# A fourth feature tile's weight sums made in device memory, and the second projection's first forms opened one product later

## The chip, the cores and the metric

One Trainium2 chip, one of its cores. The metric is device time in microseconds for one execution; the time given for a kernel is the median of several runs. The engines are TensorE (PE, matmuls; PEld is its weight loading), VectorE (DVE), ScalarE (ACT), GpSimd (POOL) and SyncE (SP, which here only issues transfers). Each has its own queue, worked through in order.

## The reference

One layer of an encoder trunk on 1024 tokens of width 1024, in float32. What matters here is the order of its parts and the gated MLP in it:

```python
hn = rmsnorm(h, norm_mix_g[i])
z = hn @ w_in[i]                       # pooling mixer columns, then q, k, v
a = pool_mixer(u, pool_w[i], pool_b[i], pool_scale[i])
o = chunk_attention(q, k, v, rel_bias[i])
h = h + jnp.concatenate([a, o], axis=-1) @ w_out[i]
hn = rmsnorm(h, norm_ffn_g[i])
up = hn @ w_up[i]                      # 1024 x 5632
gt, val = up[..., :D_FF], up[..., D_FF:]
gt = causal_dwconv(gt, conv_w[i], conv_b[i])
h = h + (jax.nn.gelu(gt, approximate=False) * val) @ w_down[i]   # D_FF = 2816
hn = rmsnorm(h, norm_ple_g[i])
gate = jax.nn.sigmoid(hn @ w_ple_gate[i] + b_ple_gate[i])
h = h + gate * (p[i] @ w_ple[i])
...
return rmsnorm(h, final_g)
```

## The kernel before

Activations lie transposed, features on the 128 partitions and tokens along the free axis. Every float32 product is made of three matmuls (`mm3`, L130 to L132): each operand is split into a high part in the matmul's type and a low part that holds the rest. `split` makes the two, the high part on ACT (L135) and the low part on DVE (L136). So any operand costs one ACT and one DVE operation before PE can use it.

The stages in order: input projections and attention (about 0 to 282 us in the profile), in which attention steps i = 0 to 66 (64 pairs of a head and a block of 128 tokens, and three to drain) are interleaved with the remaining projections, and POOL does the windowed sums of the pooling groups 2 and 3 (L458 to L472); the output projection, with `mix` for each pooling group (282 to 337); the MLP's up-projection (380 to 801); its down-projection (801 to 1005); the last gate and the norm.

**The up-projection** goes over 22 feature tiles, `fi` = 0 to 21. Each tile's product is a 2 x 2 block product in Strassen's manner: seven products numbered 1 to 7 instead of eight, each of 4 x 3 matmuls of 128x512. `steps` gives their order, 1, 5, 2, 6, 3, 7, 4 for most tiles. The seven need, as weight operands, three quarters of the weights as they are (products 1, 2, 4) and four sums of quarters (5, 6, 3, 7). Products 6 and 7 share a PSUM bank: after product 6, L858 (`u2`, on DVE) reads the bank, and product 7 accumulates on. Behind product 3, L860 and L861 finish the gate branch, and `gate` (L879 to L882) runs the convolution and GELU; behind products 7 and 4, L864 to L867 finish the value branch; `values_in` (L885, L886) multiplies the two, and SP stores the tile's result to the device-memory tensor GD (L921). The result of an even tile lies in X, of an odd tile in F.

**Where the sums come from.** For tiles 0 to 2 (`by_load`, `UP_SUMS = 3`) the four sums are made ahead of time in device memory, in the tensors SD, and each of the seven operands is one load (L755). For tiles 3 to 21 the four quarters are loaded and POOL makes the four sums in SBUF (L759, 76 operations), the sums of product 6 and 7 on top of that of product 5. `prepare` splits an operand up to four products ahead. `fetch` asks for loads into 17 buffers of 128x512: five in F and twelve in X, which is opened after the fourth product, in the place of the tile TB. For the last tile only the five in F are used.

**The sums in device memory** are made in units. A unit is one feature tile of `w_up` (unit numbers below `UP_SUMS`) or one row block of `w_down` (the eleven numbers above). `weight_sums(u, part)` has six parts with eight transfers in all: copies, and transfers that add to what lies there, which POOL issues. The first `EARLY = 8` units are made during the attention, unit u's part at step i = 7 + 6u + 2 part (`sums_due`). There, a copy of one element on POOL (L566) makes the transfers wait for a result of the attention, and all is kept behind what POOL had before in program order. The other units are made during the up-projection, with POOL issuing the adding ones and SP the copies.

**The down-projection** is a block product of the same kind, with eleven row blocks for each of seven products. Its weight operands for products 5, 6, 3 and 7 are the units of `w_down`. Its operands go through the same `split`, into a ring of buffers in B. B takes the place of X, once everything that uses X is done, which ends with the store of tile 20's result. `ready(6)` asks for the first six pairs of loads and `formed(2)` splits the first two pairs: two ACT and two DVE operations each. Both are called from `first_steps`, a hook that runs after product 6 of the last feature tile. The later pairs are asked for and split in the main loop.

**What sets the order.** PE's queue is written in program order (`manual_schedule`). For the other engines a scheduler orders the queues when the kernel is built, from what it believes to be ready and from program order; `high_priority` lifts an operation by 60 places, and `keep_in_program_order` pins one behind what its engine had before.

Of the kernel before, what the change touches and what calls it, by code (L numbers as in the profile page):

```python
# [6 lines left out]
F32 = mybir.dt.float32  # L7
# [13 lines left out]
NF = FF // P  # L21
# [62 lines left out]
def trunk(tc, xT, pT, vecs, w_qk0, w_in, w_v, bias, counts, pool_w, w_out, w_up, w_down,  # L84
# [4 lines left out]
    with tc.tile_pool(name="sb", bufs=1) as sb, \  # L89
# [6 lines left out]
        def region(z, dt):  # L96
            a, b = spans[z]
            return sb.tile([P, (b - a) * 256], dt, name=f"R{z}", tag=f"R{z}")

        Rs = [region(z, F32R) for z in range(5)]  # L100
# [3 lines left out]
        small = sb.tile([P, 80], F32, name="small")  # L104
        PS = pp.tile([P, 8, 512], F32, name="PS")
        GD = dr.tile([NF, P, SEQ], F32, name="GD")
        UP_SUMS = 3
        SD = [dr.tile([NF // 2 + UP_SUMS, P, 512], F32, name=f"SD{n}") for n in range(4)]

        b_pool = tc.tile_pool(name="b1", bufs=1)  # L110
# [431 lines left out]
        def weight(k, i, j):  # L542
            return w_down[k + NK * (j - 1), :, (i - 1) * 512:i * 512]

        def quarter(fi, q):
            return w_up[fi, q[0], :, q[1] * 512:(q[1] + 1) * 512]

        def weight_sums(u, part, copies=pool):

            s1, s2, s4, s3 = [t[u] for t in SD]  # L550
            a11, a12, a21, a22 = [quarter(u, (i, j)) if u < UP_SUMS else weight(u - UP_SUMS, i + 1, j + 1)
                                  for i in range(2) for j in range(2)]
            todo = {0: ((s1, a21, None), (s3, a21, None)), 1: ((s1, a22, ALU.add), (s3, a11, ALU.add)),
                    2: ((s2, s1, None),), 3: ((s2, a11, ALU.add),), 4: ((s4, s2, None),), 5: ((s4, a12, ALU.add),)}
            for to, src, op in todo[part]:
                tc.keep_in_program_order(pool.dma_start(to, src, accum_op=op) if op else copies.dma_start(to, src))

        EARLY = 8

        def sums_due(i, wi):  # L560

            due = [(u, part) for u in range(EARLY) for part in range(6) if 7 + 6 * u + 2 * part == i]
            if due:
# [151 lines left out]

        by_load = range(UP_SUMS)
        plain = {1: (0, 0), 2: (0, 1), 4: (1, 1)}
# [122 lines left out]
        def keep(dst, bank, scale=1.0):  # L840
            with tc.high_priority(AHEAD):
                act.activation(dst, PS[:, bank], AF.Copy, scale=scale)

        def step(fi, n):

            x, y, z, w = firsts.get(fi, (0, 1, 2, 3))
            product({1: x, 2: x, 5: z, 3: z, 6: y, 7: y, 4: w}[n], n not in (2, 3, 7))
            if n == 1 and fi != 1:
                keep(np1, x, -1.0)
            elif n == 2 and fi:  # L850
                gate0(x)
                if fi in halved:
                    gate(fi, HS[0])
            elif n == 5:
                keep(rawd if fi == 1 else V[:, HS[1]], z)
            elif n == 6:
                with tc.high_priority(AHEAD):
                    dve.tensor_tensor(u2, PS[:, y], np1, ALU.add)  # L858
            elif n == 3:
                dve.tensor_tensor(G2, PS[:, z], u2, ALU.subtract)  # L860
                dve.tensor_tensor(G2, G2, rst[:, HS[1]], ALU.mult)  # L861
                gate(fi, HS[1] if fi in halved else slice(0, SEQ))
            elif n == 7:
                dve.tensor_tensor(V[:, HS[0]], PS[:, y], np1, ALU.add)  # L864
                dve.tensor_tensor(V[:, HS[1]], V[:, HS[0]], rawd if fi == 1 else V[:, HS[1]], ALU.subtract)
            elif n == 4:
                dve.tensor_tensor(V[:, HS[0]], PS[:, w], V[:, HS[0]], ALU.add)  # L867

        def gate0(bank):
            dve.tensor_tensor(Gb[:, 2:2 + 512], PS[:, bank], rst[:, HS[0]], ALU.mult)  # L870
# [13 lines left out]
        def values_in(y):  # L884
            dve.tensor_tensor(V, V, rst, ALU.mult)  # L885
            dve.tensor_tensor(y, y, V, ALU.mult)  # L886
# [15 lines left out]
        used += [False] * 12  # L902
        Ys = (X[:, 6144:7168], Yb)

        def up(fi, hook=None):
            if fi == 0:
                pool.memset(Gb[:, 0:2], 0.0)
                gate0(firsts[0][0])
            if fi == 1:
                keep(np1, firsts[1][0], -1.0)  # L910
            for n in steps[fi]:
                step(fi, n)
                if hook and n == 6:
                    hook()
            y = Ys[fi % 2]
            due = [(EARLY + z, fi - 4 - 2 * z - z % 2) for z in range(NK + UP_SUMS - EARLY)]
            due = [(u, part) for u, part in due if 0 <= part < 6]
            if any(part % 2 for _, part in due):
                tc.keep_in_program_order(pool.tensor_copy(small[:, 78:79], y[:, 0:1]))
            values_in(y)  # L920
            tc.keep_in_program_order(sp.dma_start(GD[fi], y))  # L921
            for u, part in due:
                weight_sums(u, part, sp)
# [18 lines left out]
        def weight_sum(n, k):  # L942
            return SD[SUM_OF[n]][UP_SUMS + k]

# [9 lines left out]
        def operands(n, k):  # L954

            z = {1: k - READY, 5: k + NK - READY}.get(n, -1)
            if 0 <= z < NK:
                load_to(B12(z), gated(z, 1, 2))
            if n == 1:
                return load_to(raw_buf(), weight(k, 1, 1)), load_to(T(k), gated(k, 1, 1))  # L960
            if n in (5, 6, 3, 7):
                if n == 5:
                    load_to(B22(k), gated(k, 2, 2))
                return load_to(raw_buf(), weight_sum(n, k)), {5: T, 6: T, 3: B22, 7: B12}[n](k)
            if n == 2:
                b21[k] = load_to(raw_buf("g"), gated(k, 2, 1))
                return load_to(raw_buf(), weight(k, 1, 2)), b21[k]
            return load_to(raw_buf(), weight(k, 2, 2)), T(k)
# [23 lines left out]
        READY, FORMED, LAG, LAG_1 = 6, 2, 4, 8  # L992
        got, made = {}, [0, 0]

        def ready(upto):
            while made[0] < min(upto, len(sequence)):
                got[made[0]] = operands(*sequence[made[0]])
                made[0] += 1

        def formed(upto):  # L1000
            while made[1] < min(upto, len(sequence)):
                i = made[1]
                w_, g_ = got.pop(i)
                (split_neg if sequence[i][0] in (5, 6) else split)(g_, *g_form[i % 3])
                split(w_, *w_form[i % 4])
                behind(*sequence[i])
                if i >= LAG and sequence[i - LAG][0] != 1:
                    later_sums(*sequence[i - LAG])
                if i >= LAG_1 and sequence[i - LAG_1][0] == 1:
                    later_sums(*sequence[i - LAG_1])  # L1010
                made[1] += 1

        g_form, w_form = [], []

        def first_steps():
            x_pool.__exit__(None, None, None)
            B = b3_pool.__enter__().tile([P, 7168], F32R, name="B3")
            g_form.extend((B[:, 1024 * s:1024 * s + 512], B[:, 1024 * s + 512:1024 * s + 1024]) for s in range(3))
            w_form.extend((B[:, 1024 * s:1024 * s + 512], B[:, 1024 * s + 512:1024 * s + 1024]) for s in range(3, 7))
            Rs[0] = region(0, F32)  # L1020
            ready(READY)
            formed(FORMED)

        b3_pool = tc.tile_pool(name="b3", bufs=1)
        for fi in range(NF):
            up(fi, first_steps if fi == NF - 1 else None)
        pinned[0] = True
        for z in (1, 2, 3):
            Rs[z] = region(z, F32)
# [241 lines left out]
```

## Time and profile before

| | |
|---|---|
| median of three runs | 1139.93 us (1139.84 to 1141.75) |
| the profiled execution | 1138.89 us |
| its span, first to last instruction | 1137.1 us |
| PE busy | 1121.7 us, 99% |
| DVE busy | 891.4 us, 78% |
| ACT busy | 577.9 us, 51% |
| POOL busy | 281.5 us, 25% |
| POOL's sums of quarters, L759 | 76, in up-projection, 1.29 to 2.34 us each |
| granted TensorE clock | 0.997 |

How to read it: a line of the timeline has the start, the duration, the engine, the line of the kernel, the operation, then written and read tiles with shapes, and in brackets how long the engine was idle before it and who ended that. A line of the waits has who waited, for whom, the microseconds in total, how often and the longest. SPq is SP's queue, where transfers are issued; the time of an issue is not the time of the transfer. Matmul times overlap, since a matmul starts before the one ahead of it has ended; the distance between two starts is the pace.

### The profile page before, as it was taken

What the parts mean: (1) busy time and instruction counts of PE and PEld (TensorE: products, weight loads), DVE (VectorE), ACT (ScalarE), POOL (GpSimd) and SP (SyncE); (2) the same over time, 40 slices, a digit from 0 to 9 for tenths busy, and PEclk for the clock granted to TensorE, in tenths of its full rate; (3) what the DMA queues carried; (4) which work ended last, traced back from release to release, by engine and by line L of the source; (5) the groups of instructions that cost most, each with busy time, mean ns of one, the idle gap of its engine ahead of it and who ended that gap; (6) DMA issues with size and microseconds to landing.
All of it is one profiled execution on the core that took longest, in us unless ns stands there. A gap on an engine that the chain in (4) does not pass through costs nothing.

```text
span 1137.1 us, 15326 instructions
## 1 busy us (share of the span) xinstructions
PE 1121.7 (99%) x5517; PEld 944.6 (83%) x5517; DVE 891.4 (78%) x1371; ACT 577.9 (51%) x1001; POOL 281.5 (25%) x297
## 2 busy tenths in 40 slices
PE   9999999999999999999999999999999999999996
PEld 7988998888888878888888888887888888888886
DVE  7678878779656788989898999988896688757344
ACT  8568677765554553434343434344444567545222
POOL 0013334275002213444463555333000000000000
PEclk9999999999999999999999999999999999999998
DMA  7134756534500343142635463414673564310012
GB/s 266 38 86 114 166 118 179 122 85 130 185 14 16 122 156 102 65 140 78 172 100 157 115 167 93 102 37 127 233 269 102 167 193 159 121 48 1 1 74 75
DMA packets 63340, 133.46 MB, mean 117 GB/s; under 512 B 7392, under 2 KB 9696, under 8 KB 62816
## 3 DMA queue, kind: packets, MB, share of 16 engines
q1 hardware_dynamic: 51664, 107.25, 28.5%
q0 software_dynamic: 9856, 23.07, 11.1%
q10 hardware_dynamic: 1744, 2.17, 0.5%
q8 instruction: 43, 0.70, 0.3%
q14 instruction: 33, 0.27, 0.1%
HBM read 116.73 MB, written 45.09 MB: 142 GB/s over the span
## 4 chain that ended last, share of the span: by engine, by line
PE 88%; DVE 6%; ACT 2%; issue 2%; DMA 1%; SPq 0%; DVEq 0%; POOLq 0%; POOL 0%; ACTq 0%
PE PS L130 27%; PE PS L132 27%; PE PS L131 27%; PE PS L370 2%; PE PS L387 1%; PE PS L388 1%; DVE R L136 1%; DVE B L378 1%; ACT F L356 1%; PE PS L344 1%; PE PS L345 1%; DMA F<-in_w_qk 0%; DVE F L346 0%; DMA R<-GD 0%; PE PS L353 0%
## 5 line engine op out<-in xcount | busy, mean ns | idle before, releaser
L130 PE MATMUL PS<-R,R 128*128 128x512 f32 (+1 forms) x932 | 359.7, 386 | 2.7 <-ACT R L135 1.4
L132 PE MATMUL PS<-R,R 128*128 128x512 f32 (+1 forms) x932 | 356.0, 382 | 0.0
L131 PE MATMUL PS<-R,R 128*128 128x512 f32 x868 | 338.1, 390 | 0.5 <-DVE R L231 0.5
L130 PEld LDWEIGHTS PS<-R,R 128*128 128x128 f32 x932 | 175.2, 188 | 35.5 <-ACT R L135 3.1
L132 PEld LDWEIGHTS PS<-R,R 128*128 128x128 f32 x932 | 175.1, 188 | 34.3 <-DVE R L136 0.2
L131 PEld LDWEIGHTS PS<-R,R 128*128 128x128 f32 x868 | 163.2, 188 | 33.0 <-DVE R L231 1.7
L132 PE MATMUL PS<-B 128*128 128x512 f32 x316 | 123.3, 390 | 0.1
L130 PE MATMUL PS<-B 128*128 128x512 f32 x316 | 123.3, 390 | 0.0
L131 PE MATMUL PS<-B 128*128 128x512 f32 x316 | 123.1, 390 | 0.0
L759 POOL TENSOR_TENSOR X<-X 128x512 f32<-128x512 f32 x42 | 80.2, 1912 | 122.9 <-DVE R L136 71.2
L136 DVE TENSOR_TENSOR R<-F,R 128x512 fp32r<-128x512 f32 (+1 forms) x117 | 94.0, 815 | 19.9 <-ACT R L135 19.4
L135 ACT ACTIVATE R<-F 128x512 fp32r<-128x512 f32 (+1 forms) x121 | 72.2, 613 | 72.1 <-PE PS L131 31.1
L135 ACT ACTIVATE R<-X 128x512 fp32r<-128x512 f32 x97 | 60.6, 629 | 86.0 <-PE PS L131 58.1
L136 DVE TENSOR_TENSOR R<-X,R 128x512 fp32r<-128x512 f32 x97 | 97.3, 1004 | 0.6 <-ACT R L135 0.6
L135 ACT ACTIVATE B<-F 128x512 fp32r<-128x512 f32 (+1 forms) x94 | 60.6, 646 | 70.6 <-PE PS L131 54.4
L659 POOL TENSOR_TENSOR small<-small 128x4 f32<-128x4 f32 (+1 forms) x7 | 8.1, 1158 | 336.2 <-DVE small L658 336.2
L136 DVE TENSOR_TENSOR B<-F,B 128x512 fp32r<-128x512 f32 (+1 forms) x94 | 66.6, 712 | 26.2 <-ACT B L135 25.9
L132 PEld LDWEIGHTS PS<-B 128*128 128x128 f32 x316 | 59.3, 188 | 12.9 <-DVE B L136 0.5
L131 PEld LDWEIGHTS PS<-B 128*128 128x128 f32 x316 | 59.4, 188 | 12.3
L130 PEld LDWEIGHTS PS<-B 128*128 128x128 f32 x316 | 59.4, 188 | 12.1
L131 PE MATMUL PS<-B,R 128*128 128x256 f32 (+1 forms) x208 | 64.1, 308 | 0.0
L759 POOL TENSOR_TENSOR F<-F 128x512 f32<-128x512 f32 x20 | 38.0, 1900 | 75.0 <-DVE R L136 34.9
(178 smaller groups left out, 2092.1 us busy)
## 6 DMA issues: line engine op xcount, KB each, us to landing
SD<-in_w_down POOLq DMA_DIRECT2D x54, 256.0 KB, 4.7
X<-in_w_up SPq DMA_DIRECT2D x53, 256.0 KB, 3.4
F<-SD SPq DMA_DIRECT2D x49, 256.0 KB, 2.7
R<-GD SPq DMA_DIRECT2D x44, 256.0 KB, 5.4
F<-in_w_down SPq DMA_DIRECT2D x33, 256.0 KB, 3.4
F<-in_w_up SPq DMA_DIRECT2D x32, 256.0 KB, 3.7
GD<-X SPq DMA_DIRECT2D x11, 512.0 KB, 3.3
GD<-F SPq DMA_DIRECT2D x11, 512.0 KB, 2.9
```

Source lines behind the costliest of these rows:

```text
L130: pe.matmul(ps, ahi, bhi, start=first, stop=False, skip_group_check=more)
L131: pe.matmul(ps, ahi, blo, start=False, stop=False, skip_group_check=more)
L132: pe.matmul(ps, alo, bhi, start=False, stop=last, skip_group_check=more)
L135: act.activation(hi, src, AF.Copy)
L136: dve.tensor_tensor(lo, src, rv(hi), ALU.subtract)
L344: pe.matmul(PS[:, 4 + z, 0:320], q, K2[:, ks], start=True, stop=False)
L345: pe.matmul(PS[:, 4 + z, 0:320], q, K1[:, ks], start=False, stop=True)
L356: act.activation(S[:, 0:n], S[:, 0:n], AF.Exp, bias=s_[:, 0:1], scale=-1.0, accum_out=s_[:, 1:2])
L370: pe.transpose(pst[:, j * P:(j + 1) * P], S[:, j * P:(j + 1) * P], ident)
L378: dve.tensor_tensor(lo, pst, rv(hi), ALU.subtract)
L387: pe.matmul(O, V[:, k, h], pt[:, 0, idx], start=n_ == 0, stop=False)
L759: pool.tensor_tensor(rawu[to], rawu[a], rawu[b], op)
```

## The change

Two edits. First, `UP_SUMS` goes from 3 to 4 and `EARLY` from 8 to 9. Feature tile 3 then takes its four sums from SD, by load, as tiles 0 to 2 do, and nine units are made during the attention: four of `w_up` and, as before, five of `w_down`. The added unit's place in the row pushes the later ones on, so the attention's parts reach to step 65 where they ended at step 59. In the up-projection the same six units of `w_down` are made in the same places as before, since both constants move by one.

Second, the hook is cut in two. `first_loads` (the region and `ready(6)`) stays behind product 6 of the last feature tile; `first_forms` (the end of X, the opening of B, and `formed(2)`) goes behind product 3, the next one.

```diff
-        UP_SUMS = 3
+        UP_SUMS = 4
...
-        EARLY = 8
+        EARLY = 9
...
-        def up(fi, hook=None):
+        def up(fi, hooks={}):
...
             for n in steps[fi]:
                 step(fi, n)
-                if hook and n == 6:
-                    hook()
+                hooks.get(n, lambda: None)()
...
-        def first_steps():
+        def first_loads():
+            Rs[0] = region(0, F32)
+            ready(READY)
+
+        def first_forms():
             x_pool.__exit__(None, None, None)
             B = b3_pool.__enter__().tile([P, 7168], F32R, name="B3")
             g_form.extend((B[:, 1024 * s:1024 * s + 512], B[:, 1024 * s + 512:1024 * s + 1024]) for s in range(3))
             w_form.extend((B[:, 1024 * s:1024 * s + 512], B[:, 1024 * s + 512:1024 * s + 1024]) for s in range(3, 7))
-            Rs[0] = region(0, F32)
-            ready(READY)
             formed(FORMED)
...
-            up(fi, first_steps if fi == NF - 1 else None)
+            up(fi, {6: first_loads, 3: first_forms} if fi == NF - 1 else {})
```

## The prediction

> **What bounds the kernel now.** I read the page first, then the waits of PE, then PE's timeline where those waits fall.
>
> ```profile
> span 1137.1 us, 15326 instructions
> PE 1121.7 (99%) x5517; PEld 944.6 (83%) x5517; DVE 891.4 (78%) x1371; ACT 577.9 (51%) x1001; POOL 281.5 (25%) x297
> ...
> PE PS L130 <- ACT R L135: 1.4, 1, 1.4
> PE PS L370 <- DVE B L378: 1.0, 3, 0.5
> PE PS L130 <- DVE F L858: 0.8, 1, 0.8
> ```
>
> PE is busy for all but 15.4 us of the span, and the change adds no matmul and takes none away. So it can only win back pauses of PE, or make new ones. Of the pauses listed in the waits, two lie in the gated MLP (L130, once each), which is where the change is at work; L370's three lie in the attention. PE's timeline shows the two with their sizes.
>
> ```profile
> 411.94 0.39 PE L132 MATMUL PS<-R,R 128*128 128x512 f32 x1
> 413.12 0.47 PE L130 MATMUL PS<-R,R 128*128 128x512 f32 x1 [0.78 <-DVE F L858]
> ...
> 793.59 0.39 PE L131 MATMUL PS<-R,R 128*128 128x512 f32 x1
> 793.82 0.39 PE L132 MATMUL PS<-R,R 128*128 128x512 f32 x1
> 795.57 0.47 PE L130 MATMUL PS<-R,R 128*128 128x512 f32 x1 [1.36 <-ACT R L135]
> ```
>
> Matmuls follow each other every 0.23 us (793.59 to 793.82). The first pause is 413.12 - 411.94 - 0.23 = 0.95 us, the second 795.57 - 793.82 - 0.23 = 1.52 us. Together 2.47 us: the most that the change can win in the MLP. A measurement of this kernel can tell about 0.2% from no change, here 2.28 us of 1139.93, so winning both pauses would just show and winning one would not. The profiled run took 1138.89 us, 1.79 beyond its span; the median of the three timed runs is 1.04 us above it. I take differences from the profile and put them on the median.
>
> **The first edit in the MLP: tile 3 without sums on POOL.** The first pause stands before product 7 of feature tile 1. That product accumulates into the bank of product 6, which L858 on DVE must read first, and L858 came late:
>
> ```profile
> 399.38 1.28 DVE L880 SCALAR_TENSOR_TENSOR X<-F,vec,X 128x1024 f32<-128x1024 f32 x1
> 401.18 2.32 DVE L881 SCALAR_TENSOR_TENSOR X<-F,vec,X 128x1024 f32<-128x1024 f32 x1
> 405.46 1.23 DVE L885 TENSOR_TENSOR V<-V,F 128x1024 f32<-128x1024 f32 x1
> 407.20 2.33 DVE L886 TENSOR_TENSOR X<-X,V 128x1024 f32<-128x1024 f32 x1
> 412.29 0.68 DVE L858 TENSOR_TENSOR F<-PS,F 128x512 f32<-128x512 f32 x1
> ...
> 401.03 1.38 POOL L759 TENSOR_TENSOR F<-F 128x512 f32<-128x512 f32 x1 [13.02 <-DMA F<-in_w_up]
> 406.84 1.60 POOL L759 TENSOR_TENSOR F<-F,X 128x512 f32<-128x512 f32 x1 [4.43 <-DVE V L885]
> 418.23 1.71 POOL L759 TENSOR_TENSOR X<-X 128x512 f32<-128x512 f32 x1 [9.79 <-DVE R L136]
> ```
>
> L881 takes 2.32 us where its twin L880 takes 1.28, and L886 2.33 where L885 of the same size takes 1.23. Under both slow ones runs a sum on POOL (L759). DVE loses 1.04 + 1.10 = 2.14 us there. Whose sums are these? SP's loads tell:
>
> ```profile
> 391.09 1.76 SPq L755 DMA_DIRECT2D X<-SD  x3
> 393.21 0.98 SPq L755 DMA_DIRECT2D X<-in_w_up  x2
> 394.86 6.75 SPq L755 DMA_DIRECT2D F<-in_w_up  x5
> 404.12 3.52 SPq L755 DMA_DIRECT2D X<-in_w_up  x2
> 410.16 8.33 SPq L755 DMA_DIRECT2D X<-in_w_up  x4
> ```
>
> The last three loads from SD are products 6, 3 and 7 of tile 2; the next load is its product 4. So loads run far ahead of the products, as fast as the 17 buffers come free. What follows is tile 3's quarters (one at 393, three of the five at 394.86), then tile 4's. The sum at 401.03 is therefore the first one of tile 3 (its operand of product 5), and that at 406.84 the first of tile 4. After the change tile 3 takes seven ready loads: one at 393, the five at 394.86 and one of the two at 404.12. Its four sums go. Tile 4's second and third quarters, which its first sum needs, move into the four loads of 410.16 (410.16 + 8.33 ends at 418.49), so that sum starts after 412 instead of at 406.84. Neither sum is left between 401 and 412.
>
> DVE's queue without them: L881 ends at 402.46; the four short operations behind it and L885 (1.23) then end by 405.6, L886 runs 406.2 to 407.4, and its successors move up by 2. L858 then starts near 410.3 instead of 412.29. PE wants the bank at 411.94 + 0.23 = 412.17. The pause of 0.95 us goes with 1.2 us to spare. If POOL's next sum came back under L886, half the gain of DVE would be lost and L858 would end near 411.9 (412.97 - 1.04): still in time, so I take the whole 0.95. What is late next is the operation that tile 4's sum then meets on DVE, near the place of the sum at 418.23; DVE has caught up 2 us by then. The bounds of this term are 0 (DVE keeps its delay for some other reason) and -0.95. Tile 3's three further loads cost SP 0.33 us each and lie beside PE; its three further sums, after 437, lie beside products that do not pause today.
>
> **The second edit: forms one product later.** Moved are eight instructions, two ACT and two DVE splits for each of two forms; the loads stay behind product 6, so SP passes nothing. The second pause again stands before a product 7, that of the last tile:
>
> ```profile
> 792.86 0.63 ACT L135 ACTIVATE B<-R 128x512 fp32r<-128x512 f32 x1 [1.69 <-DMA GD<-X]
> ...
> 793.52 0.69 DVE L136 TENSOR_TENSOR B<-R,B 128x512 fp32r<-128x512 f32 x1 [1.27 <-ACT B L135]
> 794.13 0.68 DVE L136 TENSOR_TENSOR B<-F,B 128x512 fp32r<-128x512 f32 x1
> 794.74 0.69 DVE L858 TENSOR_TENSOR F<-PS,F 128x512 f32<-128x512 f32 x1
> ...
> 797.87 0.69 DVE L136 TENSOR_TENSOR B<-R,B 128x512 fp32r<-128x512 f32 x1
> 798.47 0.69 DVE L861 TENSOR_TENSOR F<-F 128x512 f32<-128x512 f32 x1
> ```
>
> The waits name ACT, but L858 ends at 795.43 just as that ACT split does. Product 3's twelve matmuls end with the one at 793.82, so product 6 was done near 791.5 and L858 could have run from there. It stood behind two splits into B, and these waited for the store of tile 20 to leave X, whose place B takes. If the splits stood behind L858, the 1.52 us would go.
>
> But does a later place in the program put them there? The queue's order is not the program's. The split at 797.87 is the third form's, which the program writes after the whole last tile, and it stands ahead of L861, which belongs to that tile's product 3. The scheduler takes whatever it believes to be ready. The new place of X's closing does not hold B back either, if the pool before it is a guide:
>
> ```profile
> 387.06 0.69 DVE L136 TENSOR_TENSOR R<-TB,R 128x512 fp32r<-128x512 f32 x1
> 387.81 1.27 SPq L755 DMA_DIRECT2D X<-SD  x3
> 390.50 0.58 ACT L842 ACTIVATE V<-PS 128x512 f32<-128x512 f32 x1
> ```
>
> X was opened where TB was closed, behind the L842 that ran at 390.50; yet the first load into X left at 387.81, as soon as the last reader of TB had ended (387.75). So I expect the two forms to stay in front of L858, and this edit to be worth 0, with ends at -1.52 and, should they instead come too late for the second projection, +0.69 for one split.
>
> **The first edit in the attention: one more unit on POOL's queue.**
>
> ```profile
> L556 POOL DMA_DIRECT2D SD<-in_w_up x18: 546/845/1163, 71.0 to 144.0; - x18
> L556 POOL DMA_DIRECT2D SD<-SD x16: 502/562/946, 85.9 to 248.5; - x16
> L566 POOL COPY small<-F x27: 174/182/1040, 70.8 to 249.1; 64x1 f32<-64x1 f32 x27
> ...
> 251.83 0.85 POOL L556 DMA_DIRECT2D SD<-in_w_down  x1 [2.56 <-DMA SD<-SD]
> 271.42 0.70 POOL L472 TENSOR_TENSOR F<-F 128x240 f32<-128x240 f32 x1
> 276.46 1.06 ACT L135 ACTIVATE B<-F 128x1024 fp32r<-128x1024 f32 x1 [2.62 <-issue]
> 277.55 0.38 ACT L393 ACTIVATE F<-PS 64x256 f32<-64x256 f32 x1
> 288.83 0.50 PE L132 MATMUL PS<-B 128*128 128x512 f32 x1
> ```
>
> A unit is six transfers from the weights and two within SD: 6 x 0.845 + 2 x 0.562 = 6.2 us of POOL. Steps 55, 57 and 59 of the attention get a second part, and 61, 63 and 65 get a part and a copy (0.18 each, 0.5 together). One landing more is waited for on the way, as at 251.83 (2.56). All of it lies ahead of or among POOL's pooling of group 3, which now ends at 272.12. It would end near 272.1 + 6.2 + 0.5 + 2.6 = 281.4. PE uses that group only in the second `mix`, after 292, so the result itself is in time. The danger is ACT's split of it at 276.46, with L393 and the splits of the output weights behind it. That ACT could start only when the last product with PT was over, so today 4.3 us of cover lie before it (272.12 to 276.46). I expect the queue's order to shift with POOL's, and take 0. The bounds are 0 and +5.0 (281.4 - 276.46).
>
> One rule speaks against the edit. The Trainium skill, page "SBUF — State Buffer", section "SBUF: two separate sides", says that a transfer issued from POOL cannot have its descriptors written while DVE runs an operation in a two-port mode. The rows of L556 bear on it: 0.845 us at the median and 1.163 at the most, so eight issues at the longest would be 8 x 1.163 = 9.3 us instead of 6.2, and the sum above would read 284.5. The trace shows no more than these 0.32 us between the median and the longest of those issues, and none held for as long as a whole operation of DVE could hold it.
>
> **Sum.** -0.95 + 0 + 0 = -0.95 us: 1139.93 - 0.95 = 1139.0.
>
> **Rivals.**
> - *Both pauses go*, -2.47: 1137.5. The forms do move behind L858. For it: L858 is ready 2 us before the first split, and whatever changes that one order wins. Against it: the third form's place, ahead of L861. Chance 0.22.
> - *ACT stands still for POOL*, slower. The place is ACT's split at 276.46: if it stays ahead of L393 while POOL ends late, every microsecond of POOL after 276.46 holds L393 and the output weights, and PE has no slack at the first `mix` (288.83, already late). At 281.4 it costs 5.0 - 0.95 = +4.0: 1144.0. It shows as slower once POOL ends after 276.46 + 0.95 + 2.28 = 279.7. Against it: a scheduler that counts the new transfers can put L393 first. Chance 0.18, two thirds of it beyond 0.2%.
> - *It does not do what it should*: the first pause stays, because another sum of POOL or another order keeps L858 late: 1139.9. Chance 0.16.
>
> **How the numbers follow.** The forecast has 0.44. Faster by over 0.2%: nearly all of the first rival, 0.21. Slower: two thirds of the second, 0.12. The rest, 0.67, is the same. The range runs from below the first rival's 1137.5 by what a small stall of the attention (L370) may give, 0.5, to the second rival's milder half, +1.7: 1137.0 to 1141.6. About 0.1 is left out on each side, and the ends of the forms' term, -1.52 and +0.69, lie inside.
>
> **What would show it.** In the changed profile: no L759 between 395 and 412, L881 and L886 of tiles 0 and 1 at 1.3 and 1.2 us, no wait of PE for L858 near 413; 72 sums instead of 76. Near 795, the two splits into B still in front of L858 and a pause of 1.5 us; if L858 stands first there, the second step is wrong. POOL's last L472 near 281, and ACT's L393 of the last values ahead of the split of group 3. A PE pause near 283 to 289 would prove the second rival.

## The result, and the profile after

The changed kernel takes 1145.01 us (median of six runs, 1144.28 to 1149.31), the kernel before 1139.87 on the same chip: a ratio of 1.0052 (over all runs, not of the medians alone) with an interval of 1.0041 to 1.0062. It is slower, by 5.1 us between the medians, where 1139.0 was forecast; that is outside the range of 1137.0 to 1141.6. The profiled execution took 1144.28 us; first the head of its page, then its waits of PE.

```profile
span 1142.5 us, 15338 instructions
...
PE 1124.0 (98%) x5517; PEld 946.2 (83%) x5517; DVE 887.3 (78%) x1371; ACT 578.7 (51%) x1001; POOL 279.3 (24%) x304
```

```profile
PE PS L130 <- ACT B L135: 3.0, 1, 3.0
...
PE PS L130 <- DVE F L858: 1.3, 1, 1.3
```

The wait near 413 is gone, the one left for L858 is the pause before the last product 7, and a new one of 3.0 us stands on top. To see where the time went I cut PE's queue at four matmuls that both kernels have, and compare the stretches between them (starts from the timelines, in us):

| stretch of PE | before | after | difference |
|---|---|---|---|
| to the first matmul of the output projection | 282.64 | 283.63 | +0.99 |
| output projection (to the first L655) | 55.08 | 60.14 | +5.06 |
| norm and up-projection (to the first matmul that reads B) | 463.41 | 462.40 | -1.01 |
| down-projection | 204.05 | 204.06 | +0.01 |

So nearly all of the loss lies in the output projection, and the MLP won what it should. The four differences add up to 5.05 us; the spans differ by 5.4, and the other 0.3 lies behind PE's last matmul, where I didn't follow it. Of the +0.99 ahead of the output projection, 0.3 was there by 9.95 us, long before the first unit at 71 us. Another 0.3 came at 269.28, where PE's L370 starts just behind the end of DVE's L378 (269.22); a split ahead of that L378 took 1.16 us instead of 0.82. The last 0.4 came from 276.14 on, where PE's L388 starts just behind the end of the next L378 (275.27 + 0.82 = 276.09), and that one is late for the reason found below.

PE's timeline of the changed kernel in the output projection (start, duration, idle time before it in brackets), and the mean granted clock (the number after POOL's count) of the four microseconds that follow the wait:

```profile
288.88 0.39 PE L132 MATMUL PS<-R,R 128*128 128x512 f32 x1
292.24 0.50 PE L130 MATMUL PS<-B 128*128 128x512 f32 x1 [2.96 <-ACT B L135]
292.57 0.40 PE L131 MATMUL PS<-B 128*128 128x512 f32 x1
293.29 0.78 PE L132 MATMUL PS<-B 128*128 128x512 f32 x1 [0.32 <-DVE B L136]
293.86 0.63 PE L130 MATMUL PS<-B 128*128 128x512 f32 x1
294.29 0.63 PE L131 MATMUL PS<-B 128*128 128x512 f32 x1
...
296.42 0.56 PE L130 MATMUL PS<-R,R 128*128 128x512 f32 x1
296.81 0.40 PE L131 MATMUL PS<-R,R 128*128 128x512 f32 x1
```

```profile
292.00:296.00 4.00, 3.44 (x9) 2.45 (x10) 3.88 (x10) 2.95 (x6) 0.00 (x0) 0.67 0.89 242
```

The pause is 292.24 - 288.88 - 0.23 = 3.13 us. The next two gaps lose 0.10 and 0.49. Then PE goes at 0.43 us a matmul instead of 0.23: the seven steps from 293.29 to 296.42 take 3.13 us where 1.61 is the pace, 1.52 lost, and the step after them 0.16. Together 5.40. Before, the same place lost 0.37 (gaps of 0.49 and 0.34 around 288.83), so 5.03 is new, against 5.06 in the table. About a third of it (1.68 us) is the clock, not the wait.

What holds the matmul of 292.24? Followed backwards through the timelines of ACT, SP, DVE and POOL of the changed kernel:

```profile
291.55 0.63 ACT L135 ACTIVATE B<-F 128x512 fp32r<-128x512 f32 x1 [4.27 <-DMA F<-in_pool_w]
...
288.75 0.33 SPq L182 DMA_DIRECT2D F<-in_pool_w  x1
...
269.74 0.68 DVE L136 TENSOR_TENSOR R<-F,R 128x512 fp32r<-128x512 f32 x1
274.45 0.44 DVE L458 TENSOR_TENSOR F<-F 128x271 f32<-128x271 f32 x1 [4.04 <-POOL F L458]
...
272.26 2.16 POOL L458 TENSOR_TENSOR F<-F 128x269 f32<-128x269 f32 x3
```

and the same places in the kernel before:

```profile
284.29 0.33 SPq L182 DMA_DIRECT2D F<-in_pool_w  x1
...
270.20 0.45 DVE L458 TENSOR_TENSOR F<-F 128x271 f32<-128x271 f32 x1
...
267.26 2.47 POOL L458 TENSOR_TENSOR F<-F 128x269 f32<-128x269 f32 x3
```

All these sums come from one line, L458, which runs on POOL for groups 2 and 3 and on DVE for groups 0 and 1. They keep their partial sums in the same two scratch tiles, T1 and T2. The four sums of each part of group 3 go back and forth between the two; group 0 needs one sum for each part and writes it to T1, which POOL's last sum still reads. Before, POOL was done with T1 at 267.26 + 2.47 = 269.73, and DVE came at 270.20. After, POOL is done at 272.26 + 2.16 = 274.42, and DVE, free at 270.42, stands still for 4.04 us. Everything behind it on DVE is late by that or a little more (the next L458, beside POOL's last operations, takes 0.93 us instead of 0.42). The load of the mixer's weights leaves right behind the DVE split that empties its buffer, 4.46 us later than before; ACT's split follows it, and PE that. DVE cannot catch up, as a stretch of time of the kernel before shows (behind the length come the busy times of PE, PEld and DVE):

```profile
272.00:300.00 28.00, 27.91 (x128) 22.71 (x127) 27.25 (x53) 17.34 (x28) 0.12 (x1) 1.00 0.63 202
```

It works 27.25 us of 28 there. An engine at 78% over the span has 0.75 us of slack in this stage.

### The profile page after: what moved, and what is told of

Same layout as the page of the kernel before. It is cut to its first block, busy times and chain, and to the rows that moved or that the text cites. A ratio compares the mean times of both kernels' runs of the same rounds, so it can differ in the third digit from the quotient of the medians.

```text
span 1142.5 us, 15338 instructions
## 1 busy us (share of the span) xinstructions
PE 1124.0 (98%) x5517; PEld 946.2 (83%) x5517; DVE 887.3 (78%) x1371; ACT 578.7 (51%) x1001; POOL 279.3 (24%) x304
## 4 chain that ended last, share of the span: by engine, by line
PE 86%; DVE 5%; POOL 3%; ACT 2%; issue 2%; DMA 1%; SPq 0%; DVEq 0%; POOLq 0%; ACTq 0%
PE PS L130 27%; PE PS L131 27%; PE PS L132 27%; POOL F L458 2%; PE PS L370 1%; PE PS L388 1%; PE PS L387 1%; DVE R L136 1%; DVE B L378 1%; ACT F L356 1%; DMA F<-in_w_qk 1%; POOL F L472 0%; DVE F L346 0%; POOL F L471 0%; PE PS L655 0%
## 5 line engine op out<-in xcount | busy, mean ns | idle before, releaser
L356 ACT ACTIVATE F<-F,small 128x640 f32<-128x640 f32 (+2 forms) x64 | 44.4, 694 | 23.0 <-DVE small L354 15.4
```

Source lines behind the costliest of these rows:

```text
L356: act.activation(S[:, 0:n], S[:, 0:n], AF.Exp, bias=s_[:, 0:1], scale=-1.0, accum_out=s_[:, 1:2])
```

## The experiments

My theory after the first reading: the ninth unit's time on POOL holds DVE at the shared scratch, and this alone makes the loss. Rivals: the transfers or their traffic cost it; the forms' new place costs something; the fourth tile by load costs something. Shares are against runs of the kernel before on the same chip, with 95% intervals.

**The change taken apart: three runs.** One keeps only the cut of the hook.

```diff
-        UP_SUMS = 4
+        UP_SUMS = 3
...
-        EARLY = 9
+        EARLY = 8
```

> The second edit alone: three tiles by load and eight units in the attention as before, the forms opened behind product 3. Theory (the scheduler places the forms by readiness, not by program position): the two splits into B still stand ahead of L858 on DVE, PE pauses about 1.5 us before the last product 7, the time is that of before, 1139.9 within 0.5. Rival (the second edit costs part of the 5 us, by splitting later): 1141 or more, with a new pause near 800.

Measured: 1139.26 us, 1.0001 (0.9992 to 1.0010). The pauses near 413 and 795 are both there, 0.98 and 1.21 us (from start to start, less 0.23). The cut is worth nothing.

The next is the kernel before with `UP_SUMS = 4` alone, so that the ninth unit is made during the up-projection.

> Four tiles by load but eight units in the attention: the last unit of w_down that the attention made moves to the up-projection. Theory (the loss comes from POOL being late for the end of the attention, which here it is not): DVE does not wait for POOL near 270, the pause near 412 goes, 0.95 us faster than before, 1138.9 within 0.7. Rival (loading the fourth tile's sums is what costs): slower than before, near 1145.

Measured: 1140.13 us, 1.0005 (0.9996 to 1.0014). The first pause went as expected, but the one near 795 grew; PE's timeline:

```profile
793.85 0.39 PE L132 MATMUL PS<-R,R 128*128 128x512 f32 x1
796.24 0.47 PE L130 MATMUL PS<-R,R 128*128 128x512 f32 x1 [2.00 <-DVE F L858]
```

2.16 us against 1.52 before. So 0.95 was won and 0.64 lost, and what is left is too small to tell. Why it grew isn't settled: in the profiles that have this pause it lies between 0.96 us (nine units alone) and 2.16, so a part of it changes from one execution to the next.

The third is the kernel before with `EARLY = 9` alone: nine units during the attention, three of `w_up` and six of `w_down`.

> Nine units in the attention but only three tiles by load, forms as before. Theory: DVE waits about 4 us for POOL at its first sum of pooling group 0 (L458), PE pauses about 3 us at the first mix and runs slowly for some us behind it, and the pause near 412 stays: about 6 us slower than before, 1146 within 1. Rival (the fourth tile's loads cost): as before, 1139.9.

Measured: 1146.38 us, 1.0061 (1.0048 to 1.0074), with DVE's wait and PE's, from its timelines:

```profile
275.62 0.44 DVE L458 TENSOR_TENSOR F<-F 128x271 f32<-128x271 f32 x1 [5.54 <-POOL F L458]
...
290.02 0.39 PE L132 MATMUL PS<-R,R 128*128 128x512 f32 x1
293.27 0.50 PE L130 MATMUL PS<-B 128*128 128x512 f32 x1 [2.87 <-ACT B L135]
```

The whole loss comes with the ninth unit in the attention, and it comes with three feature tiles of `w_up` among the nine as with four.

**POOL's time without the transfers.** The kernel before, with eight fills of a free tile on POOL behind its work on group 2, and no ninth unit.

```diff
+            if g == 2:
+                for _ in range(8):
+                    later.append(lambda: tc.keep_in_program_order(pool.memset(f(12, 640), 0.0)))
```

> The kernel before, with eight memsets of 128x640 on POOL behind its sums of group 2, pinned there: POOL time alone, no transfer added, nothing else changed; they write a bias buffer that is no longer read. Theory: POOL comes some 4 to 5 us later to the sums of group 3, DVE waits for the shared scratch, PE pauses at the first mix: slower by as much as the changed kernel or more, 1143 to 1147. Rival (the transfers themselves, by their memory traffic): no loss, 1139.9.

Measured: 1146.61 us, 1.0063 (1.0050 to 1.0077). DVE's timeline shows the same wait:

```profile
276.24 0.44 DVE L458 TENSOR_TENSOR F<-F 128x271 f32<-128x271 f32 x1 [5.57 <-POOL F L458]
```

No transfer was added and no further landing waited for: POOL's lateness is enough.

**The shared scratch taken away.** The changed kernel, with two tiles of its own for group 0's sums (lines behind it move by one).

```diff
+            S1, S2 = (f(12, 272), f(13.0625, 272)) if g == 0 else (T1, T2)
...
-                src, dst, m, lo_ = u, T1, 1, 0
+                src, dst, m, lo_ = u, S1, 1, 0
...
-                    src, dst = dst, (T2 if dst is T1 else T1)
+                    src, dst = dst, (S2 if dst is S1 else S1)
```

> The changed kernel, with a scratch of its own for the sums of pooling group 0 on DVE, so that they no longer share the two scratch tiles with POOL's sums of group 3; same transfers, same POOL work. Theory (DVE waits for POOL to leave the shared scratch, and everything behind it on DVE's queue is late): the wait near 270 goes, and with it the pause of 3 us at the first mix: 1138.9 within 1. First rival (the eight transfers slow the loads of pool_w and w_out in memory): no gain, 1144 to 1146. Second rival (POOL late for group 3 itself holds ACT's split of it): no gain, 1143 to 1146.

Measured: 1142.68 us, 1.0030 (1.0018 to 1.0041). A miss: DVE's wait is gone, yet the kernel is still 3.3 us slower than the kernel before (1139.42 on this chip). Its timelines of DVE, POOL and PE:

```profile
270.37 0.87 DVE L459 TENSOR_TENSOR F<-F 128x271 f32<-128x271 f32 x1
...
273.40 2.27 DVE L136 TENSOR_TENSOR R<-F,R 128x512 fp32r<-128x512 f32 x2
...
269.08 2.75 POOL L459 TENSOR_TENSOR F<-F 128x269 f32<-128x269 f32 x3
...
274.16 2.89 POOL L459 TENSOR_TENSOR F<-F 128x269 f32<-128x269 f32 x3
...
288.50 0.39 PE L132 MATMUL PS<-R,R 128*128 128x512 f32 x1
291.17 0.50 PE L130 MATMUL PS<-B 128*128 128x512 f32 x1 [2.27 <-ACT B L135]
```

DVE starts on time (270.37), but its sum takes 0.87 us where it took 0.45 before (270.20), and two splits take 2.27. Now POOL works until 279.35, beside DVE, instead of ahead of it. PE's pause is 2.44 us, and the clock stays at full speed behind it. ACT's split of group 3 waits for POOL here, until 279.39, but that holds nothing that ends last: DVE doesn't stand still from 268.43 until its split for the first `mix` at 291.32. From its first sum to the L446 at 282.14 it takes 11.77 us where it took 8.71 before (270.20 to 278.91). These 3.06 us, and the 0.17 by which DVE began later, are the 3.23 us by which the load of the mixer's weights leaves late (287.52). So the slow operations make the loss that is left. Two causes were possible for the slow operations: POOL beside DVE, or the new place of the scratch. Two more runs tell them apart. The control is the kernel before with the same three lines.

> The kernel before, with scratch of its own for group 0's sums on DVE, nothing else. Control for the changed kernel with its own scratch. My theory (the slow DVE operations there come from POOL working beside them, not from the new place of the scratch): 1139.9, DVE's first sum of group 0 at about 270.2 and 0.45 us long, no new pause of PE. The rival (reading or writing the new place is slow): that sum at 0.7 us or more, DVE late by 2 to 3 us, 1142.

Measured: 1139.25 us, 0.9992 (0.9983 to 1.0002), and on DVE's timeline

```profile
270.28 0.45 DVE L459 TENSOR_TENSOR F<-F 128x271 f32<-128x271 f32 x1
...
272.46 1.28 DVE L136 TENSOR_TENSOR R<-F,R 128x512 fp32r<-128x512 f32 x2
```

The place isn't slow: 0.45 and 1.28 us. In the other, the changed kernel with its own scratch, POOL's work on group 3 gives way to fills:

```diff
-                                 eng.tensor_tensor(d, x, y, ALU.add))
+                                 [eng.memset(d, 0.0) for _ in range(2)] if g == 3 else eng.tensor_tensor(d, x, y, ALU.add))
...
-            if g >= 2:
+            if g == 3:
+                for t in (src, src, u, u):
+                    eng.memset(t[:, f0:n], 0.0)
+            elif g == 2:
```

> The changed kernel with scratch of its own for group 0, in which POOL's work on pooling group 3 is left out and plain fills of the same tiles, two for a sum, stand in its place: POOL is still busy there, but reads nothing. My theory (what is left of the loss with its own scratch is POOL's reading of SBUF beside DVE's sums of two SBUF operands): DVE's sums of group 0 near 270 back at 0.45 us and its splits at 0.62, the pause at the first mix under 0.4 us, output projection 55.1, 1139.5. The rival (any work of POOL slows DVE, or DVE's queue in its new order is itself too long): the pause stays at 2 us or more, output projection 57 or more, 1142.5.

Measured: 1138.36 us, 0.9988 (0.9979 to 0.9998). Its timelines of DVE and POOL:

```profile
268.19 0.69 DVE L136 TENSOR_TENSOR R<-F,R 128x512 fp32r<-128x512 f32 x1 [0.49 <-ACT R L135]
...
270.85 0.44 DVE L459 TENSOR_TENSOR F<-F 128x271 f32<-128x271 f32 x1
...
272.74 1.29 DVE L136 TENSOR_TENSOR R<-F,R 128x512 fp32r<-128x512 f32 x2
...
268.90 0.29 POOL L473 MEMSET F<- 128x240 f32 x1
```

The order of DVE's and ACT's queues is that of the run with its own scratch, DVE is fast again, and PE has no pause at the first `mix`. But the fills were over at 269.2, sooner than the sums they stand for, so POOL was simply not there: this run clears DVE's order and shows that POOL's work beside DVE is the cause, and for these operations not whether it is POOL's reading. But two earlier operations of the same run bear on that: DVE's splits at 267.00 and 268.19 fall beside the fills (265.34 to 269.19) and take 0.69 us each, while the same two in the changed kernel with its own scratch, beside POOL's sums, took 0.81 and 1.04. They speak for the reading, but two operations are few, so it stays open. Nor do fills leave every operation of DVE alone: its L361 at 262.63, a product with one number for each partition, took 1.95 us beside them and 0.84 in the kernel before. The Trainium skill, page "SBUF — State Buffer", section "SBUF: two separate sides", says that an operation of DVE with two operands in SBUF and an operation of POOL that reads SBUF take a shared pair of ports by turns, each for its whole length. The rows agree as far as they go: the two splits beside the fills were not slowed, and a sum of 0.45 us grew by 0.42, less than one of POOL's operations there (2.75 / 3 = 0.92 us) in the run with its own scratch.

**POOL early enough.** The changed kernel with the units five steps of the attention apart instead of six, so that nine units end where eight did.

```diff
-            due = [(u, part) for u in range(EARLY) for part in range(6) if 7 + 6 * u + 2 * part == i]
+            due = [(u, part) for u in range(EARLY) for part in range(6) if 7 + 5 * u + 2 * part == i]
```

> The changed kernel with the nine units closer together in the attention: unit u's part at step 7 + 5u + 2 part, so that the last part is at step 57 and not at 65. Same transfers, same POOL work, only earlier. Theory (POOL's work late in the attention holds DVE, which has no slack from 268 to 293): POOL ends its sums of group 3 by 272 as before, no wait of DVE for POOL, no pause at the first mix, the pause near 412 gone and that near 795 kept: 1138.9 within 0.8. Rival (nine units cost wherever they lie, by memory or by POOL's total): 1143 or more.

Measured: 1140.01 us, 1.0004 (0.9995 to 1.0013). POOL and DVE:

```profile
267.12 2.49 POOL L458 TENSOR_TENSOR F<-F 128x269 f32<-128x269 f32 x3
...
272.13 0.43 DVE L458 TENSOR_TENSOR F<-F 128x271 f32<-128x271 f32 x1
```

POOL is done with the scratch at 269.61, DVE doesn't wait, its operation is short, and the output projection takes 54.70 us. The loss is gone, and the pause near 412 with it. That the median doesn't show the 0.95 us won there lies within its interval. The profiled execution lost more than that elsewhere: it reached the output projection at 285.17 instead of 282.64, and 2.29 of these 2.53 us were lost by 15.17 us, long before the first unit. PE paused there 1.37 instead of 0.72 us, and then went at 0.43 us a matmul. Is the spacing worth something by itself? The kernel before with the same edit:

> The kernel before with the units of the attention five steps apart instead of six, nothing else: eight units as before, the parts end at step 52 instead of 59. It tells whether the denser spacing is worth something by itself or only undoes what the ninth unit costs. My theory (group 0's first sum on DVE had no wait before, so POOL's ending earlier frees nothing): 1139.9, the same within 0.1%, pauses near 413 and 795 both there. The rival (DVE slowed by POOL between 268 and 276 costs time even before): the output projection 0.4 us shorter, 1139.5.

Measured: 1139.39 us, 1.0000 (0.9991 to 1.0009), with pauses of 0.99 and 1.78 us near 412 and 795. It only undoes the harm.

**The second pause.** Can a later place bring L858 to the front, if it is made to hold? The kernel before, with the DVE halves of the first two forms kept in program order behind L858; the loads and the hook stay where they were.

```diff
+        def split_behind(src, hi, lo):
+            act.activation(hi, src, AF.Copy)
+            tc.keep_in_program_order(dve.tensor_tensor(lo, src, rv(hi), ALU.subtract))
...
-                (split_neg if sequence[i][0] in (5, 6) else split)(g_, *g_form[i % 3])
-                split(w_, *w_form[i % 4])
+                fn = split_behind if i < FORMED else split
+                (split_neg if sequence[i][0] in (5, 6) else fn)(g_, *g_form[i % 3])
+                fn(w_, *w_form[i % 4])
```

> The kernel before, with DVE's halves of the first two forms pinned behind what DVE has before them in program order, which is L858; the forms stay behind product 6. Theory (the pause near 795 is L858 standing behind two splits that wait for the store of tile 20): L858 starts near 791.6, the pause of 1.5 us goes, 1138.4 within 0.6, the pause near 412 stays. Rival (something else holds product 7, ACT's split for it or its own weights): the pause stays, 1139.9.

Measured: 1138.53 us, 0.9992 (0.9983 to 1.0001). On DVE's timeline L858 now comes ahead of the splits (L991), and PE's pause near 795 is gone:

```profile
794.22 0.68 DVE L858 TENSOR_TENSOR F<-PS,F 128x512 f32<-128x512 f32 x1
795.40 0.69 DVE L991 TENSOR_TENSOR B<-R,B 128x512 fp32r<-128x512 f32 x1 [0.50 <-ACT B L990]
```

The profiled run had another pause, 1.50 us before 673.71, which no other profile shows and which I can't explain. All three together, the fourth tile by load, nine units five steps apart, and the two pinned forms:

> Both: four tiles by load, nine units closer together in the attention, and the forms behind product 6 with DVE's halves pinned behind L858. Theory: both pauses of the gated MLP go and the attention is not harmed: 1139.9 - 0.95 - 1.5 = 1137.4 within 0.8. Rival (what is won at 412 and 795 is given back, by other waits further on, as the second pause grew when the fourth tile was loaded alone): 1139 or more.

Measured: 1139.53 us, 1.0001 (0.9992 to 1.0010). A miss. The pause near 412 is gone, that near 795 is 1.24 us (793.18 to 794.65, less 0.23), and DVE's timeline says why:

```profile
793.21 0.69 DVE L136 TENSOR_TENSOR B<-F,B 128x512 fp32r<-128x512 f32 x1 [1.26 <-ACT B L135]
793.82 0.69 DVE L858 TENSOR_TENSOR F<-PS,F 128x512 f32<-128x512 f32 x1
```

With the first two forms held, an unheld split of a later form is put in front of L858. So I held four:

> Nine units with a spacing of five steps, the fourth tile by load, the forms opened behind product 6 as before, and now the DVE halves of the first four forms written behind L858. My theory (a pause goes only if nothing that the scheduler may pick earlier stands ahead of L858): no pause near 412, none near 795, nothing lost in the attention; 1139.9 - 0.95 - 1.5 = 1137.4, ratio 0.998. The rival (the pause near 795 only moves on, since the second projection's first forms then come late for PE): a pause of 0.7 to 2 us on the first product of the second projection, 1138.5 or more.

Measured: 1144.29 us, 1.0042 (1.0029 to 1.0055). The rival was right, and its price was too low. The second projection starts 1.42 us sooner than with two forms held (798.79 against 800.21), so the pause did go; but forms three and four, written behind the whole last tile, now stand behind its gate and L886. PE's timeline, and the stretch that follows:

```profile
804.27 0.39 PE L130 MATMUL PS<-B 128*128 128x512 f32 x1
808.62 0.79 PE L131 MATMUL PS<-B 128*128 128x512 f32 x1 [3.96 <-DVE B L991]
```

```profile
808.50:812.00 3.50, 3.38 (x8) 2.57 (x9) 3.08 (x6) 0.00 (x0) 0.00 (x0) 0.54 0.88 279
```

4.12 us of pause, and again a slow clock behind it (0.54). No version beats the kernel before by what can be told: the best that does all its work, two forms held alone, has an interval that still holds 1 (0.9983 to 1.0001).

## Why the prediction was wrong, step by step

**"The first edit in the MLP", -0.95: right.** From the changed kernel's timelines of DVE and POOL:

```profile
407.22 1.28 DVE L881 SCALAR_TENSOR_TENSOR X<-F,vec,X 128x1024 f32<-128x1024 f32 x1
...
412.20 1.22 DVE L886 TENSOR_TENSOR X<-X,V 128x1024 f32<-128x1024 f32 x1
...
416.31 0.68 DVE L858 TENSOR_TENSOR F<-PS,F 128x512 f32<-128x512 f32 x1
...
420.50 1.30 POOL L759 TENSOR_TENSOR X<-X 128x512 f32<-128x512 f32 x1 [26.44 <-DMA X<-in_w_up]
```

No sum before 420.50, L881 and L886 at 1.28 and 1.22, no wait at product 7, 72 sums in all. The stages ahead ended 6.05 us later, so L858 at 416.31 stands where 410.26 stood before; 410.3 was forecast. The stretch is 1.01 us shorter: 0.95 is this pause, 0.10 the one near 795 (1.52 before, 1.42 after), and the rest is small and the other way.

**"The second edit", 0: right.** The changed kernel's timelines of DVE and PE:

```profile
798.57 0.69 DVE L136 TENSOR_TENSOR B<-R,B 128x512 fp32r<-128x512 f32 x1 [0.85 <-ACT B L135]
799.18 0.68 DVE L136 TENSOR_TENSOR B<-F,B 128x512 fp32r<-128x512 f32 x1
799.78 0.68 DVE L858 TENSOR_TENSOR F<-PS,F 128x512 f32<-128x512 f32 x1
...
800.61 0.47 PE L130 MATMUL PS<-R,R 128*128 128x512 f32 x1 [1.26 <-DVE F L858]
```

The two splits stand ahead of L858 as they did; the program's order did not decide. The runs with held forms show that L858's place is what makes the pause.

**"The first edit in the attention", 0: this step failed.** The sentence was "I expect the queue's order to shift with POOL's, and take 0"; measured, +5.06 in the output projection and some 0.7 ahead of it. I had looked for who *reads* POOL's result, and found the second `mix` with time to spare. I had not looked for who next *writes* the scratch that POOL works in. That was DVE, 0.47 us behind POOL (269.73 to 270.20), on an engine without slack. The row of DVE's L458 was in the trace of before. The order of the queues did not shift: DVE's sum stayed where it was, and waited; ACT's split of group 3 stayed ahead of L393.

The rival that ends slower, "ACT stands still for POOL", had the sign, the stage and nearly the sum (1144.0), with a chance of 0.18, and the wrong waiter. From the changed kernel's timelines of ACT and POOL:

```profile
277.45 1.06 ACT L135 ACTIVATE B<-F 128x1024 fp32r<-128x1024 f32 x1 [3.02 <-PE PS L387]
...
275.94 0.69 POOL L472 TENSOR_TENSOR F<-F 128x240 f32<-128x240 f32 x1
```

ACT's split came 0.09 us behind the end of PE's last L387, as in the kernel before (0.08), since POOL's last L472 ended at 276.63 and not at 281.4: the last two parts of the ninth unit came behind the pooling, not among it. So that term was too long by half, and the wait stood elsewhere. (With its own scratch POOL ended at 279.35, and there ACT's split did wait for it, until 279.39.) The point from which the rival decides, POOL after 279.7, was far too late: DVE's slack ended at 0.47 us.

**The bound on this term**, 0 to +5.0, came out next to the 5.06 by coincidence: these are a wait of 4.04 us on DVE with no slack to absorb it, less what PE had in hand, and a price that no row of before showed, the slow clock. The prediction took PE's busy time as fixed, so that only pauses could be won or made; with the same 5517 matmuls it grew from 1121.7 to 1124.0 us.

**The rule on POOL's transfers** that I weighed made no difference. The changed kernel's instructions of L556, with durations min/median/max in ns:

```profile
L556 POOL DMA_DIRECT2D SD<-in_w_up x24: 556/840/1246, 71.3 to 164.8; - x24
```

0.840 us at the median as before (0.845), 1.246 at the most: no issue took more than 0.41 us longer than the median one.

## What to carry to other kernels

Before work is added to an engine, look up for each tile that it writes who *uses the same memory next*, results and scratch alike, and how much time lies between in the trace; a shared scratch tile is a dependency that no formula of the program shows. Read the slack of that next engine in its own stage (27.25 of 28 us here), not from its share of the span. Where the added work can be moved to a place in which its engine idles, move it first and measure both: here one step's spacing was the difference between +5.1 us and nothing that can be told.

## What the runs showed of the hardware

- **A pause of PE of some 3 us was paid for one and a half times.** After pauses of 3.02 (nine units alone), 3.08 (POOL's time alone), 3.13 (changed kernel) and 4.12 us (four forms held) matmuls went at 0.43 us instead of 0.23 for some 3 us; with nine units alone this began only 2.2 us behind the pause. After 2.44 us (own scratch) they did not. In the changed kernel the slow spell cost 1.52 + 0.16 = 1.68 us. The length of a single pause doesn't decide alone: in the profile of the nine units five steps apart the matmuls from 11.76 to 15.17 us were slow after pauses of 1.37 and 0.56 us, and with the fills in place of POOL's sums a pause of 1.99 us at the same place had no such effect. The Trainium skill, page "TensorE: Matmul & The Clock Gate", section "Part 1: The HAM clock gate", says that PE falls to half its clock after at least one idle window of about 3.4 us. The halved pace agrees; the length does not, since 2.87 us idle (nine units alone) were enough here.
- **POOL's sums beside DVE's** made DVE's sums of two SBUF operands take 0.87 us instead of 0.45, and two splits 2.27 instead of 1.28; two splits beside POOL's fills took 0.69 each, as fast as alone.
